# A two-layer hybrid decoder on one core: a Strassen pair's second raw tile loaded and summed first, w_down on the ring of two, x in one tile, and compressed scores behind the first gates

## The chip, the cores and the metric

The kernel runs on one core of one Trainium2 chip. The metric is the device time of one execution in microseconds (us). TensorE (PE) multiplies matrices into PSUM banks, VectorE (DVE), ScalarE (ACT) and GpSimd (POOL) work on elements, and SyncE (SP) issues most DMAs. Each engine takes its instructions in the order in which the program issues them; semaphores order them across engines, so an instruction that waits holds up everything behind it on its engine.

## The reference

The reference is a trunk of two layers on x of 512 tokens by 1024 channels in float32. Each layer is:

```python
h = rmsnorm(x, norm_mix)
q_a, k_a, v_a, f_a, q_b, kv_b, g_b, gate_a, gate_b = split(h @ w_in)
y_a = fox_attention(q_a, k_a, v_a, log_sigmoid(f_a + b_forget)) @ w_o_fox    # 8 heads of 64
kc, vc = compress_blocks(kc), compress_blocks(vc)   # windows of 32 with stride 16, a small MLP: 31 blocks
o_c, o_s, o_w = nsa_attention(q_b, kc, vc, ks, vs, kw, vw)   # 8 heads, 2 key/value heads
y_b = (g[0] * o_c + g[1] * o_s + g[2] * o_w) @ w_o_nsa
x = x + (sigmoid(gate_a) * y_a + sigmoid(gate_b) * y_b) @ w_out
h = rmsnorm(x, norm_mlp)
x = x + square(relu(h @ w_up)) @ w_down             # 1024 -> 4096 -> 1024
```

A last rmsnorm follows. NSA has three branches: attention to the 31 compressed blocks, to selected blocks, and to a sliding window, each with a gate of its own.

## The kernel before

Activations are held transposed, as eight tiles of 128 channels by 512 tokens. Nearly every product is computed in split precision: an operand is cut into a hi part (rounded to the matmul's type; names ending in h) and a lo part (the remainder; names ending in l), and `gemm` (L236 to L238) multiplies hi by hi, hi by lo and lo by hi. Activations get their parts in `make_u` (L258 on ScalarE, L259 on VectorE), weights in `Body.convert` (L210 on ScalarE, L211 on VectorE).

**Buffers.** `t(tag, ...)` gives out tiles from rings: a tag has a fixed number of buffers (`BUFS`: raw=2, crs=1, t2=12, kk=1, e=2, va=4 and so on), and a new tile of a tag waits until the readers of the tile that held the buffer are done. A ring's order of allocation so decides which earlier work a load waits for.

**Weights.** `order` lists every weight chunk of a layer, some 0.5 MB each, in the order of use, with a tag where it isn't `raw`. `weights` takes the next converted chunk. `convert` splits a loaded chunk and `fetch` (L194) then issues the next load on SyncE's queue, so about one chunk is loaded ahead of the one being converted. From the seventh on, the chunks of w_down (`wd2`) go through the one buffer of tag `crs`, which otherwise holds the rope tables (loaded at L898 in each layer), and so does the first of `wdn`, the part of w_down behind them.

**Start.** `first_u` loads one tile of x (L1235) into a ring of tag `t2` and splits it; the token projection of layer 0 (`token_proj`, L350 to L352) multiplies each as it comes, 12 matmuls per tile. The sums of squares for the norm run beside it: L267 on ScalarE, L277 on GpSimd.

**Attention.** `attend` interleaves the steps of attention units (scores, transposes, values) with a generator of other work, the fill, which is taken by an estimate of how long TensorE would stand. For FoX that is `fill1`, for NSA `fill2`. An NSA unit of four steps is one head in one branch (selected or window); its scores are L557 and L560, the softmax's mask, exponent and sums L547 to L572, transposes L585 with their split at L589 and L590, values L611. After a pair of heads `after` adds the compressed branch from `pc` (L965), joins the two halves (L972 on ScalarE, L973 on VectorE) and splits the result into oh (L501) and ol (L502), which the output projections read. `cmp_gen(hk)` makes the compressed probabilities for the key/value head hk in `cmp_probs`: scores for four heads, a copy, transposes (L732), a softmax on VectorE (L735, L739, L740, L743, L744, L746, L747) and transposes back (L751) into `pc[hk]`. A unit whose `ready` needs `pc[hk]` makes `attend` draw fill until it is there. `gated(m)` projects the gates m and m + 1 (L997) and multiplies them with FoX's output; `qproj` projects queries.

**MLP.** The first eight of the 32 row blocks of w_up are plain. The others are done in pairs by `Strassen`, with 7 products in place of 8. `load(g)` brings the raw blocks of pair g: r1 (block 2g + 1, that is a11 and a12) and r2 (block 2g, s1's parts). An accumulating DMA on GpSimd's queue (L1354) adds r2's second half onto its first, which makes s1; `third` loads the first half of block 2g again into s3 (L1360) and adds r1's first half to it by another accumulating DMA (L1361). Pairs of odd g take their tiles from the ring `va`, of even g from `e`, where s3 lies behind r1 in its buffer. `Strassen.convert(g)` makes s2 and s4 on VectorE (L1374, L1375) and the parts of the seven operands (L1378 on ScalarE, L1379 on VectorE); it is a generator that `unit(g - 1)` steps through between its products (L1389) and the elementwise work L1413 to L1457. Between products, `unit` also runs pieces of w_down (`down`), whose result is added to x on VectorE at L1090; that also releases the PSUM bank. Pair g + 2 is loaded at the beginning of unit g.

Of the kernel before, what the change touches and what calls it, by code (L numbers as in the profile page):

```python
# [14 lines left out]
OP = mybir.AluOpType  # L15
# [4 lines left out]
T = 512  # L20
KT = D // 128
# [122 lines left out]
class Body:  # L144
# [13 lines left out]
    def t(self, tag, shape, dt=F32, name=None):  # L158
        if tag in self.TINY:
            n, bufs = self.TINY[tag]  # L160
            o = self.offset[tag] + self.turns[tag] % bufs * n
            self.turns[tag] += 1
            v = self.tiny[:, o:o + int(np.prod(shape[1:]))]
            return v.rearrange("p (a b c) -> p a b c", a=shape[1], b=shape[2]) if len(shape) == 4 else \
                v.rearrange("p (a b) -> p a b", a=shape[1]) if len(shape) == 3 else v
        n = int(np.prod(shape[1:]))
        if tag in ("tmp", "small") and n < T:
            v = self.sb.tile([128, T], dt, name=name or tag, tag=tag, bufs=self.BUFS[tag])[:, :n]
            if len(shape) > 2:
                v = v.rearrange("p (a b) -> p a b", a=shape[1])  # L170
            if len(shape) > 3:
                raise ValueError(shape)
            return v
        return self.sb.tile(shape, dt, name=name or tag, tag=tag, bufs=self.BUFS[tag])

    def p(self, tag):
        if tag == "O":
# [648 lines left out]
    def order(self, l):  # L826

        a = self.a
        flat = lambda ap: ap.rearrange("p k c -> p (k c)")
        wb = [flat(a["wb"][l, i]) for i in range(32)]  # L830
        for c in range(4):
            s = a["wva"][l, c]
            if l == 0 and c == 0:
                yield from ((s[:, j], 512) for j in range(2))
            else:
                yield flat(s), 1024
        yield from ((flat(a["wg2"][l, c]), 576) for c in range(4))
        for i in (0, 1, 2, 3, 8, 9, 4, 5, 6, 7, 10, 11, 12, 13):
            yield wb[i], 1024
        wo = [[flat(a["wo"][l, f, m]) for m in range(4)] for f in range(2)]  # L840
        for m in range(8):
            yield wb[16 + m], 1024
            if m % 2 == 1:
                yield wo[0][m // 2], 1024
            if m in (1, 3):
                yield wb[14 + m // 2], 1024
        yield from ((wb[24 + m], 1024) for m in range(8))
        yield from ((wo[1][m], 1024) for m in range(4))
        yield from ((flat(a["wout"][l, m]), 1024) for m in range(8))
        yield from ((flat(a["wup"][l, j]), 1024) for j in range(self.PLAIN))  # L850
        yield from ((a["wd2"][l, c, m], 1024, *(("crs",) if 4 * c + m > 5 else ())) for c in range(6) for m in range(4))
        yield from ((flat(a["wdn"][l, m]), 1024, *(("crs",) if m == 0 else ())) for m in range(8))

    def layer(self, l, u):
        nc, a = self.nc, self.a
        wb = a["wb"][l].rearrange("m p k c -> m p (k c)")

        va = [self.p(t) for t in ("S", "S", "PT", "PT")]
# [75 lines left out]
        def cmp_gen(hk):  # L934
            yield from self.cmp_probs(hk, [st.get(("qb", p)) for p in range(4)])
# [72 lines left out]
                                               op0=OP.add, op1=OP.mult)  # L1008

        def fill2():  # L1010
            yield from cmp_gen(0)
            yield from gated(0)
            yield from qproj(2)
            yield from gated(2)
            yield from qproj(3)
            yield from gated(4)
            yield from cmp_gen(1)
            yield from gated(6)
            for m in range(8):
                yield from proj(24 + m, ("gb", m), lambda ps: gate_tanh(ps, ("oh", "ol")[m % 2]))  # L1020
# [48 lines left out]
    def mlp(self, l, x, u, acc, gm):  # L1069

        nc, a = self.nc, self.a
        R = None
        pend = []
        acts = []

        def act(ps):
            t = self.t("tmp", [128, T])
            nc.vector.scalar_tensor_tensor(t, ps, 0.0, R, op0=OP.max, op1=OP.mult)
            h = self.t("oh", [128, T], F32R)
            lo = self.t("ol", [128, T], F32R)  # L1080
            nc.scalar.activation(t, t, AF.Square)
            nc.scalar.copy(h, t)
            nc.vector.tensor_tensor(lo, t, h.bitcast(F32), op=OP.subtract)
            acts.append((h, lo))

        def down(c, m, w):

            ps = self.bank()
            yield from self.gemm(ps, w, 4 * (m % 2), acts[4 * c:4 * c + 4], ks=4)
            nc.vector.tensor_add(x[m], x[m], ps)  # L1090

        def downs():
            for c in range(6):
                for m in range(8):
                    if m % 2 == 0:
                        w = self.weights(a["wd2"][l, c, m // 2])
                    yield lambda: run(down(c, m, w))

        S = Strassen(self, l, x, gm)
        D = downs()  # L1100
        raws = [None] * 16
        g0 = self.PLAIN // 2
        S.load(g0)
        S.load(g0 + 1, third=False)
        for j in range(self.PLAIN):
            ps = self.bank()
            w = self.weights(a["wup"][l, j].rearrange("p k c -> p (k c)"))
            run(self.gemm(ps, w, 0, u))
            if R is None and j == 0:
                pend.append(ps)  # L1110
                continue
            if R is None:
                R, _ = self.rstd(acc, (self.turn_tag(), self.turn_tag()))
                prep = S.prepare(R)
                for p in pend:
                    act(p)
            act(ps)
            for _ in range(3):
                next(prep, None)
        conv = S.convert(g0)  # L1120
        for i in range(12):
            next(D)()
            if i < 7:
                next(prep, None)
                next(prep, None)
            elif i == 7:
                run(prep)
            else:
                next(conv, None)
                next(conv, None)  # L1130
            if i == 8:
                S.third(g0 + 1)
        run(conv)
        for g, n in zip(range(g0, 16), (2, 2, 3, 3, 4, 4, 4, 4, 4, 3, 1, 0)):
            S.load(g + 2)
            S.unit(g, D, n, acts)
        for d in D:
            d()
        u_next = []
        acts = acts[24:]  # L1140
        if l + 1 < L:
            acc = []
            self.load_small(l + 1)
            for m in range(8):
                ps = self.bank()
                w = self.weights(a["wdn"][l, m].rearrange("p k c -> p (k c)"))
                run(self.gemm(ps, w, 0, acts))
                nc.vector.tensor_add(x[m], x[m], ps)
                acc = self.sumsq(x[m], acc, m == 7)
                u_next.append(self.make_u(x[m], self.gain[:, 16 * l + 16:16 * l + 24], m))  # L1150
                nc.scalar.dma_start(self.xs[m], x[m])
        else:
            self.last(x, acts, a["wdn"][l])
        self.acc = acc
        return u_next
# [75 lines left out]
            self.nc.sync.dma_start(self.small, self.a["small"][l])  # L1231

    def first_u(self, u, k):
        x = self.t("t2", [128, T], name="x")
        self.nc.sync.dma_start(x, self.a["xT"][k])  # L1235
        u.append(self.make_u(x, self.gain[:, :8], k))
        return x

    def go(self):
        nc, a = self.nc, self.a  # L1240
# [18 lines left out]
        nc.scalar.activation(warm, ones[:, :1], AF.Exp)  # L1259
        self.xs = [self.dp.tile([128, T], F32, name=f"xs{k}") for k in range(KT)]  # L1260
        self.x_src = [a["xT"][k] for k in range(KT)]
        self.acc, u = [], []
        self.plan = deque(x for l in range(L) for x in self.order(l))
        self.loaded, self.split = deque(), deque()
# [6 lines left out]
class Strassen:  # L1271
# [67 lines left out]
    def load(self, g, third=True):  # L1339

        if g < 16:
            b = self.b
            if g % 2:
                r1, r2, s3 = (b.t("va", [128, 1024], name="raw") for _ in range(3))
                self.raw[g] = [r1, r2, s3[:, :512]]
            else:
                r1, r2 = (b.t("e", [128, 1536], name="raw") for _ in range(2))
                self.raw[g] = [r1[:, :1024], r2[:, :1024], r1[:, 1024:]]
            for m, t in zip((2 * g + 1, 2 * g), self.raw[g]):
                self.nc.sync.dma_start(t, b.a["wup"][self.l, m].rearrange("p k c -> p (k c)"))  # L1350
            r1, r2, _ = self.raw[g]
            if third:
                self.third(g)
            self.nc.gpsimd.dma_start(r2[:, :512], r2[:, 512:], accum_op=OP.add)  # L1354

    def third(self, g):

# [137 lines left out]
```

## Time and profile before

| | us |
|---|---|
| median of 3 runs (lowest to highest) | 1536.84 (1535.04 to 1539.64) |
| the profiled execution | 1535.83 |
| its span on the core | 1533.7 |
| TensorE busy in it | 1508.6 |
| VectorE busy | 1098.6 |
| ScalarE busy | 812.6 |
| GpSimd busy | 190.5 |

A matmul of 512 columns lasts 401 ns in the profile, but the next one starts some 0.23 us later, so they overlap; a gap shows as a row with idle time in brackets. In rows of a timeline the first number is the start in us from the start of the span, the second the duration, and "SPq" or "POOLq" marks an engine's DMA issues. In rows of waits the three numbers are the total, the count and the longest. A row that merges several instructions has their count behind an x, and its duration runs from the first one's start to the last one's end.

Layer 0 has FoX up to about 160 us, NSA to 358, the output projections, the plain MLP blocks and the first of w_down to about 500, then the Strassen units, and the rest of w_down; layer 1 runs through the same stages some 753 us later.

### The profile page before, as it was taken

What the parts mean: (1) busy time and instruction counts of PE and PEld (TensorE: products, weight loads), DVE (VectorE), ACT (ScalarE), POOL (GpSimd) and SP (SyncE); (2) the same over time, 40 slices, a digit from 0 to 9 for tenths busy, and PEclk for the clock granted to TensorE, in tenths of its full rate; (3) what the DMA queues carried; (4) which work ended last, traced back from release to release, by engine and by line L of the source; (5) the groups of instructions that cost most, each with busy time, mean ns of one, the idle gap of its engine ahead of it and who ended that gap; (6) DMA issues with size and microseconds to landing.
All of it is one profiled execution on the core that took longest, in us unless ns stands there. A gap on an engine that the chain in (4) does not pass through costs nothing.

```text
span 1533.7 us, 21178 instructions
## 1 busy us (share of the span) xinstructions
PE 1508.6 (98%) x7696; PEld 1263.3 (82%) x7696; DVE 1098.6 (72%) x2124; ACT 812.6 (53%) x1530; POOL 190.5 (12%) x184
## 2 busy tenths in 40 slices
PE   8999999999999999999999999999999999999997
PEld 7878888888888878888888787888888887888897
DVE  5678988877478776775647799886674977676662
ACT  6465655654454655555435556655444635555553
POOL 4000000000200222112310000000011002222122
PEclk9999999999999999999999999999999999999999
DMA  7555423136324545431546552322553254444221
GB/s 257 152 146 147 139 71 97 55 104 189 120 96 144 138 137 142 140 83 64 175 148 168 157 139 75 102 64 69 172 158 96 90 159 138 132 140 139 56 69 55
DMA packets 67575, 188.81 MB, mean 123 GB/s; under 512 B 8560, under 2 KB 9968, under 8 KB 67472
## 3 DMA queue, kind: packets, MB, share of 16 engines
q1 hardware_dynamic: 56672, 168.31, 35.5%
q0 software_dynamic: 6912, 12.59, 4.8%
q10 hardware_dynamic: 3888, 6.58, 1.2%
q8 instruction: 60, 0.98, 0.3%
q14 instruction: 43, 0.35, 0.1%
HBM read 147.53 MB, written 4.19 MB: 99 GB/s over the span
## 4 chain that ended last, share of the span: by engine, by line
PE 89%; DVE 5%; ACT 2%; DMA 2%; issue 1%; POOL 0%; SPq 0%; DVEq 0%; POOLq 0%; ACTq 0%
PE ps_mm L236 12%; PE ps_mm L238 12%; PE ps_mm L237 12%; PE ps_PT L236 3%; PE ps_PT L237 3%; PE ps_PT L238 3%; PE ps_O L1389 3%; PE ps_S L1389 3%; PE ps_mm L1389 3%; PE ps_O L611 2%; PE ps_PT L585 2%; PE ps_S L236 2%; PE ps_S L237 2%; PE ps_S L238 2%; PE ps_PT L1389 2%; PE ps_O L236 2%
## 5 line engine op out<-in xcount | busy, mean ns | idle before, releaser
L210 ACT CAST wh<-raw 128x1024 fp32r<-128x1024 f32 (+2 forms) x187 | 192.6, 1030 | 272.7 <-issue 84.7
L211 DVE TENSOR_TENSOR wl<-raw,wh 128x1024 fp32r<-128x1024 f32 (+2 forms) x187 | 224.9, 1203 | 49.1 <-ACT wh L210 44.2
L236 PE MATMUL ps_mm<-uh,wh 128*128 128x512 f32 x512 | 205.4, 401 | 0.0
L238 PE MATMUL ps_mm<-uh,wl 128*128 128x512 f32 x512 | 202.1, 395 | 0.0
L237 PE MATMUL ps_mm<-ul,wh 128*128 128x512 f32 x512 | 202.0, 394 | 0.0
L236 PE MATMUL ps_mm<-oh,wh 128*128 128x512 f32 (+1 forms) x316 | 122.9, 390 | 0.6 <-DVE x L1090 0.6
L238 PE MATMUL ps_mm<-oh,wl 128*128 128x512 f32 (+1 forms) x316 | 122.0, 386 | 0.0
L237 PE MATMUL ps_mm<-ol,wh 128*128 128x512 f32 (+1 forms) x316 | 121.9, 386 | 0.0
L238 PEld LDWEIGHTS ps_mm<-uh,wl 128*128 128x128 f32 x512 | 96.3, 188 | 21.1 <-issue 0.8
L236 PEld LDWEIGHTS ps_mm<-uh,wh 128*128 128x128 f32 x512 | 96.6, 189 | 19.6 <-DVE wl L211 1.5
L237 PEld LDWEIGHTS ps_mm<-ul,wh 128*128 128x128 f32 x512 | 96.7, 189 | 16.5
L1379 DVE TENSOR_TENSOR sl<-raw,sh 128x512 fp32r<-128x512 f32 x120 | 91.0, 766 | 25.2 <-ACT sh L1378 24.2
L1361 POOL DMA_DIRECT2D raw<-raw x24 | 21.9, 911 | 670.8 <-DVE ptl L590 238.1
L589 ACT CAST pth<-ps_PT 128x384 fp32r<-128x384 f32 (+1 forms) x96 | 49.2, 512 | 60.4 <-PE ps_PT L585 60.3
L548 ACT ACTIVATE E<-E,tiny 128x384 f32<-128x384 f32 (+3 forms) x112 | 65.7, 587 | 20.7 <-DVE tiny L547 20.1
L1378 ACT CAST sh<-raw 128x512 fp32r<-128x512 f32 x120 | 73.0, 618 | 6.8 <-PE ps_O L1389 2.7
L547 DVE CUSTOM_DVE_ANT_0 E<-ps_S,ct 128x384 f32<-128x384 f32 (+3 forms) x112 | 57.1, 513 | 25.0 <-PE ps_S L560 24.6
L236 PEld LDWEIGHTS ps_mm<-oh,wh 128*128 128x128 f32 x316 | 59.4, 188 | 12.8 <-DVE x L1090 1.0
L238 PEld LDWEIGHTS ps_mm<-oh,wl 128*128 128x128 f32 x316 | 59.4, 188 | 12.4
L237 PEld LDWEIGHTS ps_mm<-ol,wh 128*128 128x128 f32 x316 | 59.5, 188 | 10.8 <-DVE ol L502 0.4
L236 PE MATMUL ps_PT<-oh,wh 128*128 128x512 f32 x172 | 67.7, 393 | 0.0
L238 PE MATMUL ps_PT<-oh,wl 128*128 128x512 f32 x172 | 67.3, 391 | 0.0
(443 smaller groups left out, 3944.5 us busy)
## 6 DMA issues: line engine op xcount, KB each, us to landing
raw<-wb SPq DMA_DIRECT2D x64, 512.0 KB
raw<-wup SPq DMA_DIRECT2D x64, 512.0 KB
raw<-wd SPq DMA_DIRECT2D x48, 512.0 KB
raw<-raw POOLq DMA_DIRECT2D x48, 256.0 KB, 4.6
w<-w SPq DMA_DIRECT2D x32, 256.0 KB
kd<-hl SPq DMA_DIRECT2D x32, 256.0 KB
q<-hl SPq DMA_DIRECT2D x64, 128.0 KB
raw<-wo SPq DMA_DIRECT2D x16, 512.0 KB
```

What stands on the lines that cost most here:

```text
L210: nc.scalar.copy(h[:, :n], raw[:, :n])
L211: nc.vector.tensor_tensor(lo[:, :n], raw[:, :n], h[:, :n].bitcast(F32), op=OP.subtract)
L236: mm(ps, h[:, c], xh, start=start and i == 0, stop=False)
L237: mm(ps, h[:, c], xl, start=False, stop=False)
L238: mm(ps, lo[:, c], xh, start=False, stop=stop and i == ks - 1)
L547: nc.vector.tensor_tensor_reduce(e, ps, self.mask[:, T - n:], -1.0, BIG, OP.add, OP.min, mx)
L548: nc.scalar.activation(e, e, AF.Exp, bias=mx, scale=-1.0, accum_out=un["sm"][:, i:i + 1])
L585: nc.tensor.transpose(ps[:, j * 128:(j + 1) * 128], u["E"][i][:, b * 128:(b + 1) * 128], self.ident)
L589: nc.scalar.copy(h[:, e, :n], ps[:, :n])
L1378: nc.scalar.copy(h, src)
L1379: nc.vector.tensor_tensor(lo, src, h.bitcast(F32), op=OP.subtract)
L1389: mm = lambda o, w, x, **kw: self.nc.tensor.matmul(o, w, x, skip_group_check=True, **kw)
```

## The change

It has five parts, and each engine executes the same multiset of instructions as before, in another order and with other buffers.

1. `Strassen.load` takes and loads r2 (block 2g) before r1 (block 2g + 1), and issues the accumulating DMA for s1 right behind r2's load, ahead of r1's load and of s3. The order of allocation in the rings turns with it: r2 gets the buffer that r1 had. For even g, s3 still lies behind r1.
2. The chunks of w_down lose the tag `crs` and go through the ring `raw` of two, as all other weights do.
3. x is loaded into one tile of tag `kk` with room for all eight parts, in place of eight tiles of the ring `t2`.
4. In `fill2`, `gated(0)` comes ahead of `cmp_gen(0)`.
5. Nine tags (`LOCAL`) have rings of their own in each part of the program (a0, m0, a1, m1 for attention and MLP of the layers), so that their addresses may differ between parts.

```diff
+        bufs = self.BUFS[tag]
+        if tag in self.LOCAL:
+            tag += self.part
+        return self.sb.tile(shape, dt, name=name or tag, tag=tag, bufs=bufs)
+    LOCAL = "kd", "kk", "q2", "vn", "hl", "zz", "pt", "e0", "t2"
+    part = "a0"
...
-        yield from ((a["wd2"][l, c, m], 1024, *(("crs",) if 4 * c + m > 5 else ())) for c in range(6) for m in range(4))
-        yield from ((flat(a["wdn"][l, m]), 1024, *(("crs",) if m == 0 else ())) for m in range(8))
+        yield from ((a["wd2"][l, c, m], 1024) for c in range(6) for m in range(4))
+        yield from ((flat(a["wdn"][l, m]), 1024) for m in range(8))
...
     def layer(self, l, u):
+        self.part = f"a{l}"
...
         def fill2():
+            yield from gated(0)
             yield from cmp_gen(0)
-            yield from gated(0)
...
     def mlp(self, l, x, u, acc, gm):
+        self.part = f"m{l}"
...
     def first_u(self, u, k):
-        x = self.t("t2", [128, T], name="x")
+        x = self.x0[:, k]
...
+        self.x0 = self.t("kk", [128, KT, T], name="x")
...
             if g % 2:
-                r1, r2, s3 = (b.t("va", [128, 1024], name="raw") for _ in range(3))
-                self.raw[g] = [r1, r2, s3[:, :512]]
+                r2, r1, s3 = (b.t("va", [128, 1024], name="raw") for _ in range(3))
             else:
-                r1, r2 = (b.t("e", [128, 1536], name="raw") for _ in range(2))
-                self.raw[g] = [r1[:, :1024], r2[:, :1024], r1[:, 1024:]]
-            for m, t in zip((2 * g + 1, 2 * g), self.raw[g]):
+                r2, r1 = (b.t("e", [128, 1536], name="raw") for _ in range(2))
+                s3 = r1[:, 1024:]
+            r1, r2, s3 = self.raw[g] = r1[:, :1024], r2[:, :1024], s3[:, :512]
+            for m, t in zip((2 * g, 2 * g + 1), (r2, r1)):
                 self.nc.sync.dma_start(t, b.a["wup"][self.l, m].rearrange("p k c -> p (k c)"))
-            r1, r2, _ = self.raw[g]
+                if t is r2:
+                    self.nc.gpsimd.dma_start(r2[:, :512], r2[:, 512:], accum_op=OP.add)
             if third:
                 self.third(g)
-            self.nc.gpsimd.dma_start(r2[:, :512], r2[:, 512:], accum_op=OP.add)
```

More of the change, by code (lines that the diff above doesn't have):

```diff
@@ L173, in t @@
             return v
-        return self.sb.tile(shape, dt, name=name or tag, tag=tag, bufs=self.BUFS[tag])
+        bufs = self.BUFS[tag]
[4 more added lines that the diff above has]
+    part = "a0"
     def p(self, tag):
```

## The prediction

> **What bounds the kernel now.** I read the page's busy line first, then the chain by engine, then busy time by stretch, then TensorE's timeline wherever a stretch was not full.
>
> ```profile
> span 1533.7 us, 21178 instructions
> PE 1508.6 (98%) x7696; PEld 1263.3 (82%) x7696; DVE 1098.6 (72%) x2124; ACT 812.6 (53%) x1530; POOL 190.5 (12%) x184
> PE 89%; DVE 5%; ACT 2%; DMA 2%; issue 1%; POOL 0%; SPq 0%; DVEq 0%; POOLq 0%; ACTq 0%
> ```
>
> TensorE is busy 1508.6 of 1533.7 us. Its work is the same multiset of instructions after the change, so only its 25.1 us of idle time, and stretches at a lower granted clock, can be won; nothing bounds what can be lost. The stretches of 20 us in which it was not full, with one full one (520) for comparison:
>
> ```profile
> 0.00:20.00 20.00, 16.10 (x69) 13.24 (x70) 7.24 (x11) 10.74 (x16) 10.04 (x18) 1.00 0.74 242
> 180.00:200.00 20.00, 18.79 (x98) 14.80 (x96) 19.31 (x53) 12.89 (x29) 0.00 (x0) 1.00 0.15 50
> 520.00:540.00 20.00, 20.00 (x107) 17.01 (x106) 16.49 (x22) 12.44 (x23) 4.79 (x4) 1.00 0.48 135
> 540.00:560.00 20.00, 17.03 (x86) 13.92 (x85) 13.83 (x20) 11.24 (x19) 4.38 (x4) 1.00 0.48 142
> 920.00:940.00 20.00, 18.85 (x102) 15.61 (x101) 19.15 (x53) 14.78 (x34) 0.00 (x0) 1.00 0.34 95
> 1260.00:1280.00 20.00, 19.43 (x102) 16.34 (x101) 16.08 (x20) 12.81 (x22) 5.66 (x5) 1.00 0.46 127
> 1300.00:1320.00 20.00, 15.89 (x73) 13.04 (x72) 13.91 (x19) 9.40 (x17) 2.17 (x2) 0.91 0.42 112
> 1304.70:1308.20 3.50, 3.43 (x12) 2.95 (x13) 1.83 (x3) 3.21 (x7) 1.28 (x1) 0.61 0.11 44
> 1308.20:1312.00 3.80, 3.80 (x19) 3.23 (x19) 2.23 (x4) 2.24 (x5) 0.00 (x0) 0.91 0.19 24
> ```
>
> The columns are stretch, its length, busy time of TensorE, weight load, VectorE, ScalarE, GpSimd, then granted clock, DMA share and GB/s. The idle time is in three kinds of places: the start, one place in each layer's NSA stretch (180, 920), and the beginning of each layer's Strassen MLP (540; 1260 and 1300). The gaps themselves, from TensorE's timeline (in brackets the idle time before the instruction and who ended it):
>
> ```profile
> 19.75 0.50 PE L350 MATMUL ps_S<-wh,uh 128*128 128x512 f32 x1 [2.71 <-ACT uh L258]
> 183.67 0.73 PE L560 MATMUL ps_S<-kk,q 128*128 128x512 f32 x2 [1.21 <-DVE tiny L547]
> 543.73 0.50 PE L1389 MATMUL ps_O<-b,sh 128*128 128x512 f32 x1 [1.11 <-DVE x L1090]
> 551.90 0.50 PE L1389 MATMUL ps_S<-t,sh 128*128 128x512 f32 x1 [1.86 <-ACT y L1413]
> 936.35 0.74 PE L560 MATMUL ps_S<-kk,q 128*128 128x512 f32 x2 [1.15 <-DVE tiny L547]
> 1272.44 0.50 PE L1389 MATMUL ps_S<-t,sh 128*128 128x512 f32 x1 [0.56 <-DVE x L1090]
> 1304.77 0.50 PE L1389 MATMUL ps_mm<-t,sh 128*128 128x512 f32 x1 [4.11 <-DVE x L1090]
> ```
>
> Behind the last one the granted clock falls: 3.5 us at 0.61 and 3.8 us at 0.91 lose 3.5 x 0.39 + 3.8 x 0.09 = 1.7 us.
>
> **The Strassen pairs (load, r2 first).** The gaps name L1090, VectorE's release of a PSUM bank, but the cause stands ahead of it in VectorE's in-order queue: L1374 (s2 = s1 + a11) waits for the accumulating DMA that makes s1 in r2. Waits, VectorE's timeline, SyncE's issues and the chain:
>
> ```profile
> DVE s L1374 <- DMA raw<-raw: 19.5, 10, 3.7
> 542.99 0.69 DVE L1090 TENSOR_TENSOR x<-x,ps_O 128x512 f32<-128x512 f32 x1
> 546.42 0.69 DVE L1374 TENSOR_TENSOR s<-raw 128x512 f32<-128x512 f32 x1 [2.75 <-DMA raw<-raw]
> 513.16 8.72 SPq L1350 DMA_DIRECT2D raw<-wup  x2
> 528.65 9.44 SPq L1350 DMA_DIRECT2D raw<-wup  x2
> 528.65 3.77 DMA raw<-wup
> 533.10 3.33 DMA raw<-raw
> 541.79 4.61 DMA raw<-raw
> 1295.01 5.46 DMA raw<-raw
> ```
>
> The two merged SyncE rows hold four loads: g=9's r1 at 513.16, g=8's r1 at 521.55 (8.72 - 0.33 after the first), g=8's r2 at 528.65, g=9's r2 at 537.76. Each waits for a buffer. So g=9's r2 is issued at 537.8, its sum lands at 546.4, and VectorE idles 2.75 us at L1374; g=8's sum lands at 536.4, 3.33 after 533.10. After the change r2 takes the place and the buffer that r1 had: g=9's r2 goes out at 513.2, its sum is there some 25 us sooner, and r1 goes out at 537.8. Load and sum were in series (3.77 + 0.68 + 3.33 = 7.8 us for g=8); after the change, behind the late issue stands one load. L1374 waits for r1 too: for g=9 537.8 + 3.8 = 541.6 instead of 546.4, 4.8 us sooner; for g=8 528.65 + 3.8 = 532.5 instead of 536.4, 3.9 sooner. Those exceed the gaps they feed (1.11 + 1.86; VectorE idles 2.75 in front of the second). VectorE also reaches L1374 up to 0.6 us sooner, since it stands one operation earlier. Left over: 0 to 1 us, I take 0.3. Layer 0: -2.97 + 0.3 = -2.7. Layer 1 has the same order, its late sum took 5.46 us: 0.56 + 4.11 + 1.7 of clock = 6.4, less 0.4: -6.0. If the wait for r1 shortens the 4.11 only in half, 2 us and perhaps the clock loss stay.
>
> What becomes later: s3's load and sum follow r1's load; its reader (the conversion at 554.9 for g=8) is over 15 us behind the sum's new landing. GpSimd's accumulates stand ahead of other work there (ol L1457, acc L277): 0.9 us of issue each, and a wait for the load if GpSimd gets there early; GpSimd is busy 4 to 6 of 20 us, so I price it at nothing; if one such wait holds an ol that TensorE needs, it costs that wait, 1 to 4 us.
>
> **The start (x in one tile).** Before, x's loads wait for a free buffer of a ring:
>
> ```profile
> 8.28 4.57 DMA x<-xT
> 8.65 0.43 SPq L776 DMA_DIRECT2D ct<-const  x1
> 15.09 3.34 SPq L1235 DMA_DIRECT2D x<-xT  x4
> 18.98 0.73 ACT uh L258
> ```
>
> The fifth x tile is issued at 15.09 and its hi half ready at 19.71; TensorE, done with the fourth at 17.0 (19.75 - 2.71), stands 2.71 us. With one tile for all eight there is no ring: the fifth follows the constants (L776) directly, with only reuse of a DMA semaphore before it, and now also precedes the last w_va load. Behind L776 it is issued by about 9.1; a load of x under this load took 4.57, so it lands at 13.7 and its hi half is ready at 14.4 (0.73 of L258). That leaves 2.6 us to 17.0, in case the DMA engines, 0.74 busy over these 20 us, share out more thinly. Bounds: 0 (ScalarE stays as late) to -2.71; I take -2.4. The fourth w_va load now comes behind two more x tiles, at most 2 x 4.57 if nothing overlaps and about 2 us if they share; its cover is that it waits for a conversion that frees its buffer anyway. If that cover is gone, 2 us come back.
>
> **w_down on the ring of two.** Eighteen loads per layer change from a private buffer to the common ring. No gap of TensorE before hangs on them; each load is issued one conversion earlier or stays, the last ones are no longer held 200 us early. Cover: a block of 24 matmuls at 0.23 us each (rows 353.29 and 353.52 below), 5.5 us, stands between issue and use, against 3.77 us of load. Zero; if two loads queue behind a Strassen load it could be 2 us. The rings named by part (LOCAL) change addresses and the first waits of a part, whose last readers lie long before: zero.
>
> **The first gates ahead of the compressed scores.** Nothing is added, TensorE's order changes over 160-357 and 915-1100. This is the edit that can lose. VectorE is the tight engine there (19.31 and 19.15 of 20 above). Before, its chain for compressed probabilities lies between the transposes L732 and L751:
>
> ```profile
> 352.82 0.63 PE L965 MATMUL ps_O<-cp,kcz 128*128 128x256 f32 x4
> 353.29 0.40 PE L236 MATMUL ps_mm<-oh,wh 128*128 128x512 f32 x1
> 353.52 0.40 PE L237 MATMUL ps_mm<-ol,wh 128*128 128x512 f32 x1
> 178.28 0.69 DVE L735 TENSOR_TENSOR tmp<-ps_PT,ct 128x512 f32<-128x512 f32 x1 [0.22 <-PE ps_PT L732]
> 184.22 0.69 DVE L747 TENSOR_TENSOR tmp<-tmp,tiny 128x512 f32<-128x512 f32 x1
> 354.11 0.68 DVE L973 TENSOR_TENSOR o<-ps_O,tmp 64x512 f32<-64x512 f32 x1 [1.26 <-ACT tmp L972]
> 356.82 0.69 DVE L502 TENSOR_TENSOR ol<-o,oh 128x512 fp32r<-128x512 f32 x1 [0.69 <-ACT oh L501]
> ```
>
> From 178.28 to 184.91 it takes 6.6 us with other heads' work between. Both orders put 26 TensorE instructions between L732 and L751, by their rows some 6 to 6.9 us without a stall; I expect 0.25 + 0.65 in place of 1.21 (and of 1.15): -0.3. The second group's chain (some 6 us against 6.0 of cover, no gap before): 0 to 0.7, I take 0.3. At the end of the stretch, TensorE has 11 matmuls (2.5 us) between the last L965 and the first that reads the new oh; before it had 15. The last L965 ended at 353.45, oh was ready just before 356.82, ol at 357.51: 3.3 us against 2.5, and then 0.7 more for ol against two matmuls (0.5): a new gap of about 1.0. Per layer -0.3 + 0.3 + 1.0 = +1.0, less 0.3 for what the small gaps share (a stall at one place gives VectorE time for the next): +0.7, twice +1.4. Bounds: -1.2 (all goes) to +3 (VectorE's 0.7 us spare in 20 makes each of the three places cost one more operation of 0.69) per layer.
>
> A page of the Trainium skill speaks against such an order: "TensorE: Matmul & The Clock Gate", section "A second HAM failure mode: psum-queue depth-cycling", says that short idle stretches of TensorE between groups of matmuls, from cycling through PSUM banks, can swing its clock between half and full. The trace does not bear it out for short gaps: around those of 2.71, 1.21 and 1.11 + 1.86 the clock reads 1.00, and only after 4.11 is it lower. By the trace the sum stays; by the rule each new gap could cost a half-rate stretch like the 1.7 us above.
>
> **Sum.** -2.4 - 2.7 - 6.0 + 1.4 = -9.7 us. The profiled execution took 1535.83 (span 1533.7), 1.0 below the median 1536.84: from it 1526.1, as a median 1527.1. I forecast 1527.
>
> **Rivals.**
> 1. The r1 wait replaces the r2 wait. For: L1374 reads both, and r1 is now issued at the old late time. Against: one DMA of 3.8 us stands behind that time in place of 7.8 us. If half the Strassen gain (4.4) stays away: 1531.5. Chance 0.12.
> 2. The start does not move, because loads share the DMA engines (0.74 busy) or ScalarE's queue keeps uh late. Against: 14.4 against 17.0. Time 1529.5. It lies inside the forecast's own range; chance 0.1.
> 3. Slower: the NSA order. If VectorE, without slack, is passed by TensorE at more than the three places, each of the 16 units (8 heads, 2 branches) of a layer waits for an L547 as at 183.67. It decides when the loss per layer passes (11.1 + 4.6) / 2 = 7.9 us, six or seven gaps of 1.2. At 0.6 us per unit, half of that gap: 9.6 x 2 = 19.2, less 11.1: 1545. For: 19.31 of 20 busy. Against: only one gap in each layer's stretch before, at the same amount of work. Chance 0.13.
> 4. Half clock after short gaps: three new gaps per layer, 1.7 each, 10.2: 1537. The rows of clock 1.00 speak against it. Chance 0.04.
> 5. The loads are not earlier after all (another release holds the same buffer) and the NSA edit is neutral: gain only at the start, 1534. Chance 0.06.
>
> **How the numbers follow.** Forecast with rival 2: 0.65, from 1522 to 1531. Low end: everything goes (-2.7 - 3.0 - 6.4 - 2.4 = -14.5, 1522.3), and 2 for layer-1 order: 1520. High end: rival 1 with NSA at its bound (+6 for +1.4) is 1536, and part of 3: 1540. About 0.3%, 4.6 us, is what a measurement of this kernel can tell from no change, so faster means below 1532.2: 0.65 plus most of rival 1 is 0.73. Same takes the rest of 1, 4 and 5: 0.14. Slower, rival 3: 0.13.
>
> **What the changed profile would show.** Right: L350 at about 17 with under 0.5 us before it; no wait of L1374 on raw<-raw above 1 us, and at most short ones on raw<-wup; no L1389 gap above 1 us at about 540 and 1295, granted clock 1.00 there; gaps of about 1 us at the two L236 that read oh at 356 and 1112. Wrong: L1374 waiting 2 us or more for raw<-wup; several L560 or L751 gaps between 160 and 340; GpSimd's accumulate waiting ahead of an ol that TensorE wants.

## The result and the profile after

The changed kernel takes 1525.84 us (median of 6 runs, 1525.23 to 1526.51), the kernel before 1537.54 us (1535.04 to 1539.64, 6 runs): a ratio of 0.9925 with a 95% interval of 0.9912 to 0.9937, that is 9.7 to 13.5 us faster. The forecast was 1527, range 1520 to 1540.

The lines of its code have moved: by 7 up to the attention stages and by 8 to 10 behind them. So L1374 of before is L1384, L1389 is L1399, L1090 is L1099, L1354 and L1361 are L1362 and L1371, L258 is L265, L547 and L560 are L554 and L567, and L236 to L238 are L243 to L245. The page's first lines, and then the stretches that were not full, in the columns of the prediction:

```profile
span 1523.5 us, 21173 instructions
PE 1508.0 (99%) x7696; PEld 1263.1 (83%) x7696; DVE 1099.1 (72%) x2124; ACT 809.8 (53%) x1530; POOL 192.1 (13%) x184
```

```profile
0.00:20.00 20.00, 18.03 (x78) 15.21 (x79) 8.00 (x12) 12.78 (x19) 11.35 (x19) 1.00 0.84 291
180.00:200.00 20.00, 19.97 (x99) 16.16 (x98) 18.54 (x44) 10.87 (x23) 0.00 (x0) 1.00 0.17 54
340.00:360.00 20.00, 19.13 (x94) 15.35 (x93) 12.50 (x24) 8.66 (x16) 1.88 (x2) 1.00 0.74 237
540.00:560.00 20.00, 19.72 (x100) 16.39 (x99) 15.50 (x20) 12.08 (x21) 5.21 (x6) 1.00 0.54 130
1100.00:1120.00 20.00, 19.13 (x87) 15.29 (x86) 13.70 (x21) 7.48 (x11) 0.86 (x1) 1.00 0.65 203
1280.00:1300.00 20.00, 18.94 (x96) 15.54 (x96) 17.19 (x22) 12.43 (x23) 7.14 (x7) 1.00 0.55 146
```

TensorE is busy nearly as long as before (1508.0 against 1508.6 us); of the 10.2 us by which the span is shorter, 9.6 are idle time. The gaps that are left in these stretches, from TensorE's timeline (that of 355.37 comes again at 1105.46 in layer 1), then VectorE's wait for the sum, and its first operation on pair 9, ahead of which it stood 2.75 us at 546.42 before:

```profile
17.71 0.50 PE L357 MATMUL ps_S<-wh,uh 128*128 128x512 f32 x1 [0.87 <-ACT uh L265]
355.37 0.73 PE L243 MATMUL ps_mm<-oh,wh 128*128 128x512 f32 x2 [0.87 <-ACT oh L508]
356.10 0.50 PE L244 MATMUL ps_mm<-ol,wh 128*128 128x512 f32 x1
547.42 0.50 PE L1399 MATMUL ps_S<-t,sh 128*128 128x512 f32 x1 [0.28 <-ACT y L1423]
1284.83 0.50 PE L244 MATMUL ps_O<-ol,wh 128*128 128x512 f32 x1 [0.66 <-POOL ol L1467]
1297.05 0.50 PE L1399 MATMUL ps_mm<-t,sh 128*128 128x512 f32 x1 [0.40 <-DVE x L1099]
```

```profile
DVE s L1384 <- DMA raw<-raw: 6.2, 2, 3.3
```

```profile
539.68 0.69 DVE L1384 TENSOR_TENSOR s<-raw 128x512 f32<-128x512 f32 x1
```

VectorE waits for the sum in r2 (raw<-raw) 6.2 us instead of 19.5, and no longer where TensorE would feel it: the two waits left are at 489.54 and 1239.98, before pair 6 of each layer, and TensorE has no gap behind them. In layer 0 the gaps of 1.11 and 1.86 us have become 0.28, in layer 1 those of 0.56 and 4.11 have become 0.66 and 0.40, and the granted clock behind them is 1.00. In the NSA stretch of each layer the gap before the scores (1.21 and 1.15 us) is gone and 0.87 at its end is new. The start keeps 0.87 of 2.71.

### The profile page after: what moved, and what is told of

Its sections match the earlier page's. It is cut to its first block, busy times and chain, and to the rows that moved or that the text cites. A ratio compares the mean times of both kernels' runs of the same rounds, so it can differ in the third digit from the quotient of the medians.

```text
span 1523.5 us, 21173 instructions
## 1 busy us (share of the span) xinstructions
PE 1508.0 (99%) x7696; PEld 1263.1 (83%) x7696; DVE 1099.1 (72%) x2124; ACT 809.8 (53%) x1530; POOL 192.1 (13%) x184
## 4 chain that ended last, share of the span: by engine, by line
PE 87%; DVE 3%; ACT 2%; issue 1%; DMA 1%; POOL 0%; DVEq 0%; SPq 0%; POOLq 0%; ACTq 0%
PE ps_mm L243 12%; PE ps_mm L244 12%; PE ps_mm L245 12%; PE ps_O L1399 3%; PE ps_S L1399 3%; PE ps_PT L243 3%; PE ps_PT L244 3%; PE ps_PT L245 3%; PE ps_mm L1399 3%; PE ps_PT L1399 2%; PE ps_O L618 2%; PE ps_PT L592 2%; PE ps_S L243 2%; PE ps_S L244 2%; PE ps_S L245 2%; PE ps_O L244 2%
## 5 line engine op out<-in xcount | busy, mean ns | idle before, releaser
L243 PE MATMUL ps_mm<-uh,wh 128*128 128x512 f32 x512 | 204.4, 399 | 0.0
L245 PE MATMUL ps_mm<-uh,wl 128*128 128x512 f32 x512 | 202.3, 395 | 0.1
L243 PE MATMUL ps_mm<-oh,wh 128*128 128x512 f32 (+1 forms) x316 | 123.2, 391 | 2.0 <-ACT oh L508 1.7
L245 PE MATMUL ps_mm<-oh,wl 128*128 128x512 f32 (+1 forms) x316 | 122.4, 387 | 0.0
L1389 DVE TENSOR_TENSOR sl<-raw,sh 128x512 fp32r<-128x512 f32 x120 | 97.1, 818 | 30.2 <-ACT sh L1388 30.1
L245 PEld LDWEIGHTS ps_mm<-uh,wl 128*128 128x128 f32 x512 | 96.3, 188 | 20.9 <-issue 0.8
L243 PEld LDWEIGHTS ps_mm<-uh,wh 128*128 128x128 f32 x512 | 96.7, 189 | 19.3 <-DVE wl L218 1.5
L1362 POOL DMA_DIRECT2D raw<-raw x24 | 21.2, 885 | 696.4 <-DMA x<-xs 241.3
L554 DVE CUSTOM_DVE_ANT_0 E<-ps_S,ct 128x384 f32<-128x384 f32 (+3 forms) x112 | 57.4, 515 | 31.7 <-PE ps_S L567 30.4
L243 PEld LDWEIGHTS ps_mm<-oh,wh 128*128 128x128 f32 x316 | 59.3, 188 | 14.4 <-ACT oh L508 2.6
L245 PEld LDWEIGHTS ps_mm<-oh,wl 128*128 128x128 f32 x316 | 59.5, 188 | 12.2
L243 PE MATMUL ps_PT<-oh,wh 128*128 128x512 f32 x172 | 67.7, 394 | 0.0
L245 PE MATMUL ps_PT<-oh,wl 128*128 128x512 f32 x172 | 67.3, 392 | 0.0
```

The lines of the kernel that those rows point to most:

```text
L243: mm(ps, h[:, c], xh, start=start and i == 0, stop=False)
L245: mm(ps, lo[:, c], xh, start=False, stop=stop and i == ks - 1)
L554: nc.vector.tensor_tensor_reduce(e, ps, self.mask[:, T - n:], -1.0, BIG, OP.add, OP.min, mx)
L1389: nc.vector.tensor_tensor(lo, src, h.bitcast(F32), op=OP.subtract)
```

## The experiments

Each of the first four parts was first made alone in the kernel before (the rings named by part, the fifth, were not); then the pairs' part was taken apart, and the places that were left were tried in the changed kernel. Ratios are to the kernel before, run beside it.

| kernel | median us | ratio (95% interval) |
|---|---|---|
| pairs_only: new `load` alone | 1527.82 | 0.9932 (0.9919 to 0.9945) |
| order_only: gates first alone | 1537.74 | 1.0001 (0.9992 to 1.0011) |
| xtile_only: x in one tile alone | 1535.11 | 0.9988 (0.9976 to 1.0) |
| wdown_only: w_down on the ring alone | 1537.59 | 0.9997 (0.9987 to 1.0008) |
| sum_only: sum ahead of the third load | 1537.52 | 0.9998 (0.9988 to 1.0008) |
| first_late_sum: r2 first, sum written last | 1525.75 | 0.9918 (0.9903 to 0.9933) |
| buffers_only: allocation turned, r1 loaded first | 1537.1 | 0.999 (0.9978 to 1.0002) |
| loads_only: r2 loaded first, allocation of before | 1525.69 | 0.9919 (0.9906 to 0.9933) |
| after_start: changed kernel, early sums on VectorE | 1525.17 | 0.9913 (0.9896 to 0.9929) |
| after_fill092: changed kernel, fill rate 0.92 | 1521.66 | 0.989 (0.9876 to 0.9905) |
| after_scores_first: changed kernel, scores first again | 1524.86 | 0.9914 (0.99 to 0.9927) |
| scores_first_092: the same with rate 0.92 | 1525.97 | 0.9923 (0.9909 to 0.9936) |

### The parts alone

pairs_only has the new `load` as in the diff shown with the change, and nothing else of it.

> The kernel before with only the new load of the Strassen pairs (r2 first, its sum at once, buffers turned). Theory A (the stalls of VectorE at L1374 make the gaps of the Strassen stages): TensorE's gaps of 1.11 and 1.86 us in layer 0 and of 4.11 us with its 1.7 us of lower clock in layer 1 go but for some 0.3 to 1 us each layer; the start and the two gaps of 1.21 and 1.15 us stay. The time falls by 8.0 us, ratio 0.9948. Theory B (part of that gain came from the w_down loads going through the common ring, which changes the order on SyncE's queue): the time falls by 5 us or less, ratio 0.9967 or above.

order_only:

```diff
+            yield from gated(0)
             yield from cmp_gen(0)
-            yield from gated(0)
```

> The kernel before with only the first gates ahead of the compressed scores. Theory A: in each layer the gap of 1.2 us before L560 goes and one of 0.9 us opens at the end of the NSA stretch, where the first matmul waits for the new oh, with 0.2 us more for ol: within 0.5 us of before, ratio 1.000. Theory B (the order is worth something because VectorE is relieved in the whole stretch): 2 us or more faster, ratio below 0.9987.

xtile_only:

```diff
-        x = self.t("t2", [128, T], name="x")
+        x = self.x0[:, k]
...
+        self.x0 = self.t("kk", [128, KT, T], name="x")
```

> The kernel before with only x in one tile. Theory A: TensorE's gap of 2.71 us at the start falls to 0.9 us, nothing else changes: 1.8 us faster, ratio 0.9988. Theory B (the 0.9 us left are the DMA engines' share-out with the rest of the change): the gap falls to below 0.3 us: 2.5 us faster.

wdown_only:

```diff
-        yield from ((a["wd2"][l, c, m], 1024, *(("crs",) if 4 * c + m > 5 else ())) for c in range(6) for m in range(4))
+        yield from ((a["wd2"][l, c, m], 1024) for c in range(6) for m in range(4))
```

and the same for `wdn`.

> The kernel before with only w_down's chunks on the ring of two. Theory A: none of the waits that TensorE sees hangs on those loads: within 0.5 us of before, ratio 1.000, and the gaps of the Strassen stages stay at 1.11, 1.86 and 4.11 us within 0.5 us. Theory B (these loads move the pairs' loads on SyncE's queue): the gaps change by over 1 us, up or down.

The pairs' part alone gives 10.4 us by the ratio (8.5 to 12.5), somewhat more than the 8.0 of theory A. Its gaps moved as theory A has it (0.25 us in layer 0, 0.45 and 0.46 in layer 1), and theory B falls: w_down's loads have no share in it, and alone they change nothing. The order is worth nothing by itself; its gaps moved as expected, 0.87 us at 356.86 us in place of 1.21 us earlier. x in one tile gives 1.8 us with an interval that reaches to 0 (0 to 3.7).

The profiles of these kernels show what one profile of before could not: the same code has other gaps in other executions. The start of pairs_only, order_only and wdown_only is that of before, and so are the Strassen stages of order_only and, but for w_down's loads, of wdown_only. From their timelines:

```profile
18.96 0.70 PE L350 MATMUL ps_S<-wh,uh 128*128 128x512 f32 x1 [2.19 <-ACT uh L258]
```

```profile
552.85 0.60 PE L1389 MATMUL ps_S<-t,sh 128*128 128x512 f32 x1 [2.80 <-ACT y L1413]
1307.19 0.59 PE L1389 MATMUL ps_mm<-t,sh 128*128 128x512 f32 x1 [3.80 <-DVE x L1090]
```

```profile
17.72 0.50 PE L350 MATMUL ps_S<-wh,uh 128*128 128x512 f32 x1 [0.95 <-ACT uh L258]
551.73 0.80 PE L1389 MATMUL ps_S<-t,sh 128*128 128x512 f32 x1 [3.30 <-ACT y L1413]
1307.62 0.80 PE L1389 MATMUL ps_mm<-t,sh 128*128 128x512 f32 x1 [4.67 <-DVE x L1090]
```

The first fence is pairs_only, the second order_only, the third wdown_only. The start's gap without the x tile lies anywhere from 0.89 to 2.74 us over eight profiles (mean 1.71), so the 2.71 of before was near the top. The second gap of layer 0, 1.86 in before, is 1.77 to 3.30 over six profiles with the old loads (mean 2.48), so it was near the bottom.

### Which half of the new load counts

The new `load` turns three things: the order of the loads, the order of allocation, and the place of the sum. sum_only moves the sum:

```diff
+            self.nc.gpsimd.dma_start(r2[:, :512], r2[:, 512:], accum_op=OP.add)
             if third:
                 self.third(g)
-            self.nc.gpsimd.dma_start(r2[:, :512], r2[:, 512:], accum_op=OP.add)
```

> The kernel before, with only the accumulating DMA for s1 issued ahead of the third load and its sum; r1 is still loaded before r2, from the buffers of before. Theory A (s1 is late because r2's load is issued late): the sum still has to wait for r2, so the gaps of the Strassen stages (about 1.1, 2 to 3 and 4 us) stay within 0.5 us and the time within 1 us, ratio 1.000. Theory B (the sum is late because it stands behind s3's on GpSimd's queue): most of the 10 us of the pairs' part is gained, ratio below 0.996.

first_late_sum has the new loads and allocation, but the sum is the last line of `load`, as before:

> The kernel before with r2 loaded first and the buffers turned, but the sum for s1 issued last, behind s3's, as before. Theory A (load and sum must both come early, because GpSimd's queue is in order and s3's sum waits for r1): the sum for s1 now follows r1's load (about 541.6 us for pair 9) and s3's sum, and lands at about 547 instead of 546.4 us, so nothing is gained, ratio 1.000 with the gaps of before or up to 1 us longer. Theory B (the early load of r2 is what counts): the gaps fall as with the whole part, ratio about 0.993.

buffers_only turns allocation and sum, with the loads in the old order:

```diff
+                r2, r1, s3 = (b.t("va", [128, 1024], name="raw") for _ in range(3))
...
+                r2, r1 = (b.t("e", [128, 1536], name="raw") for _ in range(2))
+                s3 = r1[:, 1024:]
...
+            for m, t in zip((2 * g + 1, 2 * g), (r1, r2)):
```

> The kernel before with the buffers of r1 and r2 turned as in the pairs' part and the sum written right behind r2's load, but r1 loaded first; the order of instructions on the engines is that of before. Theory A (only both together let r2 be early, because SyncE's queue is in order): r1 now waits for the buffer that comes free last (about 537.8 us for pair 9) and r2 stands behind it, so the sum lands no earlier than 546 us; gaps as before or up to 1 us longer, ratio 1.000 to 1.001. Theory B (the turned buffers alone give the gain): ratio about 0.993.

loads_only is the reverse: r1 is allocated first as before, and the loop runs over `zip((2 * g, 2 * g + 1), (r2, r1))`.

> The kernel before with r2 loaded first and its sum right behind, but r1 and r2 in the buffers of before; the order of instructions on every engine is that of the pairs' part. Theory A: r2 still waits for the buffer that comes free last, and r1 now stands behind it on SyncE's queue; the sum lands at about 546 us as before, ratio 1.000 to 1.001 and the gaps stay. Theory B (the order of the loads, or the order of the engines' instructions that comes with it, gives the gain): ratio about 0.993.

Theory A of both first_late_sum and loads_only fell: either gives the whole gain (0.9918, 0.9919), while sum_only and buffers_only give none. What divides the four is the order of the two loads, so of the three edits that is the one that counts.

The other two edits were not tested by this, though. In the traces, every engine of sum_only and buffers_only executes the operations of the kernel before in the same order, and every engine of loads_only and first_late_sum those of pairs_only (addresses are not in the traces). The four runs repeat two programs: the place of the sum and the order of allocation left no mark on what was built, and what they would be worth in a program that did follow them stays open. Theory B of sum_only, the sum held up behind s3's, is answered by the trace of before itself, where GpSimd issues the sum of pair 9 (L1354) ahead of s3's (L1361), 4.0 us behind r2's load at 537.76:

```profile
541.79 0.88 POOL L1354 DMA_DIRECT2D raw<-raw  x1 [6.48 <-DVE y L1432]
542.54 1.04 POOL L1361 DMA_DIRECT2D raw<-raw  x1
```

The exchange of the loads also brings the build to another order of operations on VectorE, ScalarE and GpSimd in the Strassen stages (L1374 of pair 9 now stands ahead of L1090). No run separates that from the earlier landing.

Two things that I had read from the source are not so in the built program. First, a buffer is not tied to the order of allocation. From SyncE's timeline of loads_only, then of buffers_only:

```profile
512.58 7.47 SPq L1350 DMA_DIRECT2D raw<-wup  x2
527.66 0.33 SPq L1350 DMA_DIRECT2D raw<-wup  x1
535.87 0.33 SPq L1350 DMA_DIRECT2D raw<-wup  x1
```

```profile
515.33 8.72 SPq L1350 DMA_DIRECT2D raw<-wup  x2
530.82 9.76 SPq L1350 DMA_DIRECT2D raw<-wup  x2
```

In loads_only the row at 512.58 holds r2 of pairs 9 and 8, and r1 of both follows at 527.66 and 535.87. In buffers_only the first row holds r1 of both, and r2 follows at 530.82 and 540.25. The load that comes first gets the buffer that is free, whatever the source allocates first. Second, the place of a DMA on an engine's queue isn't that of its line. In first_late_sum, where the source writes the sum (L1353) behind s3's (L1360), GpSimd's timeline has it first:

```profile
526.04 0.88 POOL L1353 DMA_DIRECT2D raw<-raw  x1 [4.70 <-DVE x L1090]
534.69 0.88 POOL L1360 DMA_DIRECT2D raw<-raw  x1 [1.28 <-PE ps_mm L1388]
```

So this run did not test a late sum, since the sum wasn't late; whether one would cost the gain stays open.

### What was left

after_start puts the early sums of squares on VectorE:

```diff
-        (nc.vector if last else nc.gpsimd).tensor_tensor(o, s, acc[0], op=OP.add)
+        (nc.vector if last or early else nc.gpsimd).tensor_tensor(o, s, acc[0], op=OP.add)
...
-                    self.acc = self.sumsq(x, self.acc, 2 * c + j == KT - 1)
+                    self.acc = self.sumsq(x, self.acc, 2 * c + j == KT - 1, c < 3)
```

and the same for the first two tiles.

> The changed kernel with the sums of the squares of the first six x tiles on VectorE instead of GpSimd. Theory A (the 0.87 us left at the start come from ScalarE's queue: its squares and, behind them, the fifth uh wait for GpSimd's sums of 1.3 to 1.8 us each): the gap falls to below 0.3 us, 0.6 to 0.9 us faster than the changed kernel. Theory B (the DMA engines set it): the gap stays at 0.9 us.

The gap at the start is gone in its profile: the row of L357 that was at 17.71 us starts at 16.73, 0.22 behind the row ahead of it. In time it is 0.7 us, within the intervals of the two kernels, so its price is not told. The cause shows in ScalarE's rows of the changed kernel:

```profile
14.90 0.63 ACT L274 ACTIVATE sq<-x 128x512 f32<-128x512 f32 x1 [1.91 <-POOL acc L284]
16.93 0.72 ACT L265 ACTIVATE uh<-x,tiny 128x512 fp32r<-128x512 f32 x1 [1.40 <-POOL acc L284]
```

The second row is the fifth hi half. Its tile was issued at 5.33 us, but it stands behind a square (L274), and each waits for GpSimd's sum of squares. A second sign of this cause: in after_fill092, after_scores_first and scores_first_092 the build puts the fifth hi half one square earlier on ScalarE, and TensorE has no gap there, with the sums left on GpSimd. In after_fill092:

```profile
13.39 0.71 ACT L265 ACTIVATE uh<-x,tiny 128x512 fp32r<-128x512 f32 x1
```

after_fill092 changes one number, after_scores_first undoes the order, scores_first_092 does both:

```diff
-    NSA_FILL = 0.95
+    NSA_FILL = 0.92
```

> The changed kernel with the rate at which fill is drawn in the NSA stretch at 0.92 instead of 0.95. By the order of instructions, 16 instead of 11 TensorE instructions then stand between the last product of the compressed branch and the first reader of the new oh. Theory A (cover is what the gap of 0.87 us and the 0.2 us behind it lack): both go in each layer, 1.5 to 2 us faster than the changed kernel, unless a gap before L567 comes back. Theory B (VectorE's load over the stretch sets the end): the gap stays or moves, within 0.5 us.

> The changed kernel with the compressed scores ahead of the first gates again. Theory A (that part is a trade of one gap for another): the gap of 1.2 us before L567 is back in both layers and the 0.9 us and 0.2 us at the end of the NSA stretch go; within 1 us of the changed kernel, ratio to before 0.992 to 0.9935. Theory B (the part carries 2 us or more of the gain): ratio 0.994 or above.

> The changed kernel with the compressed scores ahead of the first gates again and the fill rate at 0.92 instead of 0.95. Theory A (with the end of the stretch covered by the fill rate, what the new order is worth is the gap before L567 alone): slower than the changed kernel at the rate 0.92 (1521.7 us) by the 1.2 us of that gap in each layer, some 2 to 3 us: 1524, ratio 0.991. Theory B (the lower rate alone gives the 4 us): 1522, ratio 0.9895.

after_fill092 is the fastest kernel of this study, 4.2 us below the changed one. Its windows at the end of the stretch are full, and the scores have no gap either:

```profile
180.00:200.00 20.00, 19.98 (x103) 16.22 (x102) 18.54 (x45) 10.98 (x23) 0.00 (x0) 1.00 0.17 55
340.00:360.00 20.00, 20.00 (x98) 16.45 (x97) 12.77 (x19) 8.69 (x13) 1.88 (x2) 1.00 0.75 227
1100.00:1120.00 20.00, 20.00 (x90) 16.32 (x89) 16.84 (x24) 8.03 (x12) 1.74 (x2) 1.00 0.46 154
```

The two ends account for 2 x 0.87 plus some 2 x 0.27 for ol, 2.3 us; theory A had expected 1.5 to 2. The profile's other 1.3 us are 0.87 at the start, where this build has the other order on ScalarE, and 0.66 at 1284.83, where one execution of each cannot tell whether the rate has a part in it, less 0.3 elsewhere. With the scores first the lower rate gains nothing (1525.97 against 1524.86), for there no gap stood at the end, and the one before the scores stays:

```profile
181.39 0.49 PE L567 MATMUL ps_S<-kka,q2a 128*128 128x512 f32 x1 [1.08 <-DVE tiny L554]
932.10 0.50 PE L567 MATMUL ps_S<-kka,q2a 128*128 128x512 f32 x1 [1.08 <-DVE tiny L554]
```

So at the rate 0.92 the new order is worth 4.3 us, more than the 2 to 3 expected: these two gaps are 2.2 of it, the rest is not settled. At 0.95 it is worth nothing that can be told (the intervals of 0.9914 and 0.9925 overlap). Part 4 needs the other rate to pay.

## Why the prediction was right, point by point

**What bounds the kernel** held: idle time of TensorE and stretches at a lower clock were won, and they were won in the places named. The number was helped by errors that cancel: by the two profiles the terms are -2.7 and -5.3 for the pairs, -1.8 for the start and -0.1 for the order, -9.9 in all against -9.7, with layer 1 and the start 0.7 and 0.6 too large and the order 1.5 too dear.

**The Strassen pairs.** The step that L1374 waits for the sum in r2, whose load is issued late, is what the profiles of before and after show, and exchanging the loads brought the gain in three kernels (pairs_only, first_late_sum, loads_only). Forecast -2.7 in layer 0 and -6.0 in layer 1; by the two profiles -2.97 + 0.28 = -2.7, and -4.67 - 1.7 + 0.66 + 0.40 = -5.3. The cause given for it, that r2 takes r1's place "and the buffer", was half right: the load's place brings the buffer with it, and the allocation does nothing. "Left over: 0 to 1 us" held (0.28 and 1.06), with two causes. In layer 0, VectorE's L1385 behind the sum takes 1.74 us instead of 0.69, beside a GpSimd operation (below). In layer 1 it is what I had priced at nothing with a cover: "if one such wait holds an ol that TensorE needs". GpSimd's timeline, which had the accumulate of s3 directly ahead of ol:

```profile
1282.57 0.89 POOL L1371 DMA_DIRECT2D raw<-raw  x1 [1.97 <-DVE s L1384]
1283.18 1.59 POOL L1467 TENSOR_TENSOR ol<-y,oh 128x512 fp32r<-128x512 f32 x1
```

It cost 0.66 us in that execution.

The term that was mis-sized is the clock. I priced the loss behind the 4.11 us gap alone and took the shorter gaps as free, because one profile showed a clock of 1.00 behind 1.86 and 2.71 us. Windows of 3.5 us from the end of a gap, in order_only (2.80 us), wdown_only (3.30) and pairs_only (2.19 at the start):

```profile
552.80:556.30 3.50, 3.45 (x11) 2.95 (x12) 2.19 (x3) 2.93 (x7) 1.28 (x1) 0.54 0.02 5
```

```profile
551.70:555.20 3.50, 3.47 (x11) 2.99 (x12) 2.03 (x3) 2.74 (x6) 1.28 (x1) 0.50 0.02 5
```

```profile
18.90:22.40 3.50, 3.44 (x8) 2.71 (x9) 3.07 (x3) 3.50 (x7) 2.09 (x2) 0.53 0.90 307
```

Each loses 3.5 x 0.46 to 0.50, 1.6 to 1.75 us. In four of the six profiles with the old loads layer 0 pays this too. By the six, the stages lose on average 1.15 + 2.48 + 1.04 in layer 0 and 0.56 + 4.12 + 1.4 in layer 1, 10.75 us; less the 1.3 that stay, 9.4, against 10.4 and 12.5 (10.3 to 14.5) measured for pairs_only and loads_only, two runs of one program, and -8.7 in the sum. The profiled execution of before was a kind one, 1535.83 us against a median of 1537.54.

**The start.** Forecast -2.4, measured -1.84 by the profiles and 1.8 (0 to 3.7) by time. The failed step is "it lands at 13.7 and its hi half is ready at 14.4": the fifth tile was issued in time (at 5.33 us), but its hi half is made at 16.93, behind squares that wait for GpSimd. This was the bound "ScalarE stays as late", not the value taken. The reading of before had the same fault: there too, as in seven of the eight old starts, the fifth hi half waited last for GpSimd's sum and not for its own late load. In before that chain began with the fourth tile. ScalarE's rows of before for the fourth and the fifth hi half:

```profile
12.87 0.73 ACT L258 ACTIVATE uh<-x,tiny 128x512 fp32r<-128x512 f32 x1 [2.38 <-DMA x<-xT]
18.98 0.72 ACT L258 ACTIVATE uh<-x,tiny 128x512 fp32r<-128x512 f32 x1 [1.37 <-POOL acc L277]
```

From one to the other it takes 6.1 us, through a weight conversion, squares and sums. In the changed kernel the fourth tile's load is issued at 4.02 instead of 8.28, its hi half starts at 10.68, 2.2 us sooner, and the fifth follows 6.2 us behind it, at 16.93. So by these two profiles the gain came from x in one tile, but through the fourth load. Since the start of before varies by 1.8 us from one execution to the next, its average is better taken over all profiles: 1.71 of gap and 0.58 of clock (three of the eight old starts have the half rate behind them, losing 1.65, 1.54 and 1.47 us) less 0.88 for the two new starts with this order on ScalarE (0.87 and 0.89), 1.4 us.

**w_down** at zero held (0.9997).

**The order.** Forecast +0.7 per layer. The new gap at the end came as forecast (0.87 and some 0.27 for ol, against "about 1.0"), and the scores' gap went altogether, where 0.25 + 0.65 were expected to stay, and 0.3 at the second group; VectorE is 18.54 of 20 us busy there instead of 19.31. So it is -1.21 + 1.14 = -0.1 per layer.

**The rivals.** Rival 1, the wait for r1 in place of the wait for r2, is not seen: L1384 waits for raw<-wup 1.2 us in all, in three places. Rival 2 came true in part, by ScalarE and not by the DMA engines. Rival 3 and rival 5 fell. Rival 4, half clock after short gaps: the clock is 1.00 in every window of the changed kernel quoted above, with gaps of up to 0.87 us. The rule of the Trainium skill weighed there was too wide for these gaps, but a gap need not be 4.11 us long either.

**The signs.** No L1389 gap above 1 us, the clock of 1.00 and the gaps of about 1 us behind the new oh came as named. Two signs of being right did not: L350 has 0.87 us before it, not under 0.5, and L1374 still waits for raw<-raw, 2.92 and 3.27 us before pair 6 (1.42 and 2.35 before), where it costs TensorE nothing. One sign of being wrong came true, the accumulate ahead of an ol, for 0.66 us.

## What to carry to other kernels

When an in-order engine waits for a load followed by work on the loaded tile, load first what has the longer way to go; here exchanging two loads was worth nearly the whole change (0.9932 and 0.9919 alone, 0.9925 with the rest), since it moved load and sum (7.8 us in series) out of the late issue. One profile of before does not price a gap: executions with the same order of operations differed by a factor of two in the same place (before, sum_only and buffers_only: 2.71, 1.25 and 2.74 us at the start), and a lower clock came with most of the longer ones. And a line's place in the source says little where the build lays out buffers and queues; read it from the issues in the trace, and count a variant as a test of its edit only when its trace shows another order than the kernel it varies.

## What the runs showed of the hardware

The granted clock fell behind TensorE gaps from 1.83 us on, to a mean of 0.50 to 0.72 over 3.5 us, but not behind every one: 2.71 us at the start of before and 1.86 us in its layer 0 left it at 1.00, 1.83 us at the start of first_late_sum did not. The two timeline rows and the window of the latter:

```profile
18.73 0.50 PE L350 MATMUL ps_S<-wh,uh 128*128 128x512 f32 x1 [1.83 <-ACT uh L258]
21.12 0.63 PE L350 MATMUL ps_PT<-wh,uh 128*128 128x512 f32 x1
```

```profile
18.70:22.20 3.50, 3.48 (x9) 2.76 (x10) 3.11 (x3) 3.50 (x6) 2.13 (x2) 0.56 0.91 297
```

The second row's matmul lasts 0.63 us instead of 0.40. The Trainium skill, "TensorE: Matmul & The Clock Gate", section "What's actually happening", says that the clock is halved after at least one idle window of some 3.4 us, with windows that run freely. The stretch of 3.5 us at half rate and the chance in it agree with that; gaps of 1.83 to 3.3 us that are enough do not, and the measurement decides.

A VectorE addition of two tiles in SBUF takes 0.69 us, and 1.74 where GpSimd had begun an operation on two tiles in SBUF just before:

```profile
540.76 1.30 POOL L1467 TENSOR_TENSOR ol<-z,oh 128x512 fp32r<-128x512 f32 x1
```

```profile
540.88 1.74 DVE L1385 TENSOR_TENSOR s<-s,raw 128x512 f32<-128x512 f32 x1
```

It ends at 542.62, 0.56 us behind GpSimd's end at 542.06, as if it had stood until then. "SBUF — State Buffer" of the Trainium skill, section "SBUF: two separate sides", says that such a VectorE operation and a GpSimd operation that reads SBUF lock each other out for a whole instruction; the trace agrees. It is 1.05 us in the chain ahead of the 0.28 us gap of layer 0.
